# Weight tiles that hold 512 rows of two blocks, and a matmul order that changes block every time

## The chip, the cores and the metric

The kernel runs on one core of a Trainium2 chip. The metric is device time of one execution in microseconds. The engines that matter are TensorE (PE in the profile; its weight loads are listed apart as PEld), VectorE (DVE), ScalarE (ACT), and SyncE (SP), which issues the DMAs.

## The reference, cut to what matters

Two layers of a decoder trunk over 256 positions of width 2048, in float32. What the change touches are the large products of a 256-row activation with a weight matrix:

```
u = rms_norm(x, g_mix);  cq, ckv+rope key, xb, yb, gate_a, gate_r = split(u @ w_in)   # 2048 -> 9280
attn = latent attention(cq, ckv);  rec = gated linear recurrence(xb, yb)
x = x + (sigmoid(gate_a) * attn + sigmoid(gate_r) * rec) @ w_out                     # 2048 -> 2048
x = x + relu(rms_norm(x, g_mlp) @ w_up)^2 @ w_down                                    # 2048 -> 8192 -> 2048
x = x + sigmoid(rms_norm(x, g_ple) @ w_ple_gate) * (p @ w_ple_proj)                   # 2048 -> 2048
```

The result is the final RMSNorm of x after both layers. All weights are used once.

## The kernel before, in words

Activations are stored with features on the 128 partitions and the 256 positions along the free axis, so a product is built from blocks of 128 input rows by 128 output features. An output block is a tile of 128 features x 256 positions in PSUM, summed over 16 blocks of input rows (k = 0 to 15). Float32 accuracy is made of three passes: every weight and every activation is split into a high part, rounded to the matmul's input format, and the low remainder. For each k the helper `mm3` (L219 to L223) issues high weight x high activation (L221), high weight x low activation (L222), low weight x high activation (L223). Each of these is one weight load of 128 x 128 and one matmul with 256 moving columns. The activation buffers bufA and bufB hold, for each k, the high and the low part side by side.

Weights come from HBM as "halves" of 128 x 1024 float32, 512 KB each: one output block by 8 input-row blocks (half s = 0 has k = 0 to 7, half s = 1 has k = 8 to 15). A half goes through four steps. `load` (L102 to L105) issues its DMA on SP into one of six raw buffers, up to eight halves ahead. `split_half` (L116) has ACT copy it to a high tile (L122) and DVE subtract that to get the low tile (L126); there are three buffers of each. `half` (L204) hands the pair to the matmuls and pushes the later halves forward; it also places background jobs of ACT and DVE by an estimate of engine times (E, `work`). `mm_half` (L226) then issues its 24 matmuls, calling `need` for each k, so that the activation block is there.

`mm_pair` (L255) makes two output blocks, t = 0 and t = 1, in the two 256-column parts of one PSUM bank. Its four halves run in the order (t, s) = (0,0) (0,1) (1,0) (1,1). At the first pair of a product, `crossed` swaps the middle two, so that both blocks do k = 0 to 7 before either needs k = 8. Between halves stand hooks, which issue small matmuls of the norms: `root` (L502, tiles `ms`, eight or fewer matmuls of one column) and `spread` (L551, tiles `rb`, a broadcast of the norm factors). The pairs that are not made this way are the last of each product, made by `mm_apart`, the rope key (`mm_tile`), and the small per-head products (tiles k, v, q, qr, lru, pp).

The order of every engine is written out by the program as it runs on the host; there is no scheduler behind it. Stages in a layer: c (compressed q and kv), kr, eight groups of xb, yb, gr, ga and attention, out, then four times up and down, then pg (the last gate).

The lines around the change:

```
        nc.sync.dma_start(out=t, in_=wu[h])                                        # L104
            mm3(o, hi[:, c], lo[:, c], act[0][:, k, 0, :], act[0][:, k, 1, :], first and k == 0, k == 15, shared)  # L234
            t, s = (i % 2, i // 2) if crossed else (i // 2, i % 2)                 # L260
```

## Time and profile before

| | |
|---|---|
| median of 3 runs | 2925.97 us (2925.73 to 2928.0) |
| the profiled execution | 2925.61 us, its span 2923.8 us |
| TensorE busy | 2898.5 us, 99% of the span, 24800 matmuls |
| VectorE, ScalarE busy | 1860.8 us (64%), 1536.2 us (53%) |
| DMA | 535.23 MB, mean 183 GB/s |

The profiled execution spends 1.8 us outside the span that the profile shows. In the profile, matmuls overlap: one lasts about 0.28 us from its start to its end, and the next starts some 0.11 us after it. What a matmul costs is therefore read from the distance of two starts, or from a count over a stretch, not from its length. The busy share of PE says only that a matmul is nearly always in the pipe.

### The profile page before, as it was taken

The page shows a single profiled execution, that of the slowest core. Times are in us where ns is not written, and L with a number is a line of the kernel's source. Part 1 is how long each engine was busy: PE and PEld are TensorE (multiplying, and loading weights), DVE is VectorE, ACT ScalarE, POOL GpSimd, SP SyncE. Part 2 cuts the span into 40 slices and gives each one's busy share as a digit, 9 for nine tenths or more (in the row PEclk, how much of TensorE's full clock was granted, in tenths as well). Part 3 has the DMA queues.
Part 4 walks back from the last instruction along what each step waited for, and adds up shares of the span by engine and source line. Part 5 has one row for each costly group of instructions (what it writes and reads, how often), then busy time and mean ns, then how long its engine had stood idle before and what let it go on. Part 6 is the DMA issues. An engine that isn't in the chain of part 4 may idle for free. (4 is left out here: it accounts for less than half of the span.)

```text
span 2923.8 us, 58376 instructions
## 1 busy us (share of the span) xinstructions
PE 2898.5 (99%) x24800; PEld 2893.3 (99%) x24800; DVE 1860.8 (64%) x2420; ACT 1536.2 (53%) x2050; POOL 8.9 (0%) x17
## 2 busy tenths in 40 slices
PE   8999999999999999999999999999999999999998
PEld 8999999999999999999999999999999999999998
DVE  7877777765455554556758777777654555555565
ACT  5666666644344443444546666665443444434445
POOL 0000000000000000000000000000000000000000
PEclk9999999999999999999999999999999999999999
DMA  6555555555555555555555555555555555555553
GB/s 236 172 179 175 170 177 177 177 195 185 185 187 187 188 187 187 189 186 186 194 182 172 173 174 175 179 180 176 193 187 185 186 187 187 188 188 190 186 183 130
DMA packets 146998, 535.23 MB, mean 183 GB/s; under 512 B 16560, under 2 KB 16816, under 8 KB 146736
## 3 DMA queue, kind: packets, MB, share of 16 engines
q1 hardware_dynamic: 146736, 531.50, 55.2%
q8 instruction: 194, 3.18, 0.4%
q14 instruction: 68, 0.56, 0.0%
HBM read 529.33 MB, written 2.10 MB: 182 GB/s over the span
## 5 line engine op out<-in xcount | busy, mean ns | idle before, releaser
L122 ACT ACTIVATE hi<-raw 128x1024 fp32r<-128x1024 f32 x1004 | 1065.3, 1061 | 1358.5 <-PE down L222 412.0
L126 DVE TENSOR_TENSOR lo<-raw,hi 128x1024 fp32r<-128x1024 f32 x1004 | 1229.2, 1224 | 863.7 <-ACT hi L122 862.2
L221 PE MATMUL down<-bufB,hi 128*128 128x256 f32 x1024 | 287.7, 281 | 0.0
L222 PE MATMUL down<-bufB,hi 128*128 128x256 f32 x1024 | 287.7, 281 | 0.0
L223 PE MATMUL down<-bufB,lo 128*128 128x256 f32 x1024 | 287.7, 281 | 0.0
L221 PE MATMUL down<-bufA,hi 128*128 128x256 f32 x1024 | 287.7, 281 | 0.0
L222 PE MATMUL down<-bufA,hi 128*128 128x256 f32 x1024 | 287.7, 281 | 0.0
L223 PE MATMUL down<-bufA,lo 128*128 128x256 f32 x1024 | 287.7, 281 | 0.0
L221 PE MATMUL up<-bufA,hi 128*128 128x256 f32 x1024 | 287.7, 281 | 0.0
L221 PE MATMUL up<-bufB,hi 128*128 128x256 f32 x1024 | 287.7, 281 | 0.0
L223 PE MATMUL up<-bufA,lo 128*128 128x256 f32 x1024 | 287.5, 281 | 0.0
L223 PE MATMUL up<-bufB,lo 128*128 128x256 f32 x1024 | 287.5, 281 | 0.0
L222 PE MATMUL up<-bufA,hi 128*128 128x256 f32 x1024 | 287.5, 281 | 0.0
L222 PE MATMUL up<-bufB,hi 128*128 128x256 f32 x1024 | 287.5, 281 | 0.0
L222 PEld LDWEIGHTS down<-bufB,hi 128*128 128x128 f32 x1024 | 196.6, 192 | 0.0
L222 PEld LDWEIGHTS down<-bufA,hi 128*128 128x128 f32 x1024 | 196.6, 192 | 0.0
L222 PEld LDWEIGHTS up<-bufB,hi 128*128 128x128 f32 x1024 | 196.4, 192 | 0.0
L222 PEld LDWEIGHTS up<-bufA,hi 128*128 128x128 f32 x1024 | 196.4, 192 | 0.0
L221 PEld LDWEIGHTS up<-bufA,hi 128*128 128x128 f32 x1024 | 192.2, 188 | 0.0
L221 PEld LDWEIGHTS up<-bufB,hi 128*128 128x128 f32 x1024 | 192.2, 188 | 0.0
L223 PEld LDWEIGHTS up<-bufA,lo 128*128 128x128 f32 x1024 | 192.2, 188 | 0.0
L221 PEld LDWEIGHTS down<-bufB,hi 128*128 128x128 f32 x1024 | 192.2, 188 | 0.0
(551 smaller groups left out, 7839.1 us busy)
## 6 DMA issues: line engine op xcount, KB each, us to landing
raw<-wu SPq DMA_DIRECT2D x1004, 512.0 KB, 3.4
y<-rows SPq DMA_DIRECT2D x4, 512.0 KB, 4.0
x<-xT SPq DMA_DIRECT2D x3, 512.0 KB, 8.3
x<-xT SPq DMA_DIRECT2D x2, 256.0 KB, 4.9
praw<-pT SPq DMA_DIRECT2D x2, 256.0 KB, 4.7
parT<-par SPq DMA_DIRECT2D x1, 184.0 KB, 2.4
rope_w<-pos SPq DMA_DIRECT2D x1, 128.0 KB, 3.6
gf<-gfin SPq DMA_DIRECT2D x1, 8.0 KB, 8.3
```

Source lines behind the costliest of these rows:

```text
L122: A.activation(hi, src, AF.Copy)
L126: V.tensor_tensor(out=lo, in0=src, in1=f(hi), op=ALU.subtract)
L221: T.matmul(o, lhsT=wh, rhs=ah, start=start, stop=False, skip_group_check=shared)
L222: T.matmul(o, lhsT=wh, rhs=al, start=False, stop=False, skip_group_check=shared)
L223: T.matmul(o, lhsT=wl, rhs=ah, start=False, stop=stop, skip_group_check=shared)
```

## The change

A raw tile of a pair no longer holds one block by 8 k. It holds both blocks by 4 k: columns 0 to 511 are k = 4i to 4i+3 of block t = 0 and columns 512 to 1023 the same k of block t = 1, for i = 0 to 3. The weights lie in HBM as before; a table, `plan`, says from which two halves each tile is taken, so a tile of a pair is fetched by two DMAs of 128 x 512 (256 KB, rows of 2 KB) in place of one of 128 x 1024 (512 KB, rows of 4 KB). Tiles that are not of a pair are loaded as before. `mm_both` takes the place of `mm_half` in `mm_pair`: for each k it issues six matmuls, high x high, high x low, low x high, each first for t = 0 and then for t = 1, so that the sum written and the weights loaded change at every matmul, and two matmuls after each other read the same activation. `crossed` is gone from the matmul side.

```diff
     def load(h):
         t = wraw.tile([P, 1024], F32, tag="raw", name=f"raw{h}")
-        nc.sync.dma_start(out=t, in_=wu[h])
+        for src, c, n, at in plan[h]:
+            nc.sync.dma_start(out=t[:, at:at + n], in_=wu[src, :, c:c + n])
         raws[h] = t
...
+    def pairs(n, crossed=False):
+
+        for _ in range(n):
+            b = len(plan)
+            for i in range(4):
+                plan.append(tuple(
+                    (b + (2 * (i // 2) + t if crossed else 2 * t + i // 2), 512 * (i % 2), 512, 512 * t) for t in range(2)
+                ))
+            crossed = False
...
+    def mm_both(ps, act, i):
+
+        hi, lo = half()
+        for kk in range(4):
+            k = 4 * i + kk
+            need((act[1], k))
+            ah, al = (act[0][:, k, w, :] for w in range(2))
+
+            for n, (w, a) in enumerate(((hi, ah), (hi, al), (lo, ah))):
+                for t in range(2):
+                    T.matmul(
+                        ps[:, t * S:(t + 1) * S], lhsT=w[:, (4 * t + kk) * P:(4 * t + kk + 1) * P], rhs=a,
+                        start=k == n == t == 0, stop=k == 15 and n == 2, skip_group_check=True,
+                    )
+            E["P"] += 0.656
...
-    def mm_pair(name, key, act, hooks=(), crossed=False):
+    def mm_pair(name, key, act, hooks=()):
 
 
         ps = mm_bank(name, key)
         for i in range(4):
-            t, s = (i % 2, i // 2) if crossed else (i // 2, i % 2)
-            mm_half(ps[:, t * S:(t + 1) * S], act, s, t == 0, True)
+            mm_both(ps, act, i)
             if i < len(hooks) and hooks[i] is not None:
                 hooks[i]()
```

On PE, at the first pair of the product out in layer 0, the last matmuls that wait for the newest activations (k = 14 and 15 of bufB). Before, they stand in the third of the pair's four weight tiles, hi_7052:

```order
L221 MATMUL out_0_7051<-bufB,hi_7052 128x256 [waits Activation_49]
L222 MATMUL out_0_7051<-bufB,hi_7052 128x256 [waits DVE_49]
L223 MATMUL out_0_7051<-bufB,lo_7053 128x256
L221 MATMUL out_0_7051<-bufB,hi_7052 128x256 [waits Activation_49]
L222 MATMUL out_0_7051<-bufB,hi_7052 128x256 [waits DVE_49]
L223 MATMUL out_0_7051<-bufB,lo_7053 128x256
L221 MATMUL out_0_7051<-bufB,hi_7088 128x256
```

In the changed program they stand in the fourth, hi_7237 (equal neighbours are one row with a count; names do not tell the block):

```order
L284 MATMUL out_0_7199<-bufB,hi_7237 128x256 [waits Activation_49]
L284 MATMUL out_0_7199<-bufB,hi_7237 128x256
L284 MATMUL out_0_7199<-bufB,hi_7237 128x256 [waits DVE_49]
L284 MATMUL out_0_7199<-bufB,hi_7237 128x256
L284 MATMUL out_0_7199<-bufB,lo_7238 128x256 x2
L284 MATMUL out_0_7199<-bufB,hi_7237 128x256 [waits Activation_49]
L284 MATMUL out_0_7199<-bufB,hi_7237 128x256
L284 MATMUL out_0_7199<-bufB,hi_7237 128x256 [waits DVE_49]
L284 MATMUL out_0_7199<-bufB,hi_7237 128x256
L284 MATMUL out_0_7199<-bufB,lo_7238 128x256 x2
```

Counted from 0 within the pair's 96 matmuls, the last one that waits (for the low part of k = 15) was number 70 and is now number 92.

On SP, the start of the program. Before, x (the input) and the first weight halves raw_95 and raw_99 are issued so; a wait for a DMAHW semaphore is one for an earlier DMA:

```order
L298 DMA x<-xT 128x512
L104 DMA raw_95<-wu 128x1024
L301 DMA x<-xT 128x512
L301 DMA x<-xT 128x1024
L104 DMA raw_99<-wu 128x1024
L301 DMA x<-xT 128x1024 x2
L304 DMA gf<-gfin 128x16 [waits DMAHW0_49]
L104 DMA raw_140<-wu 128x1024 [waits DMAHW1_49]
```

In the changed program each weight tile takes two issues:

```order
L351 DMA x<-xT 128x512
L142 DMA raw_95<-wu 128x512 x2
L354 DMA x<-xT 128x512
L354 DMA x<-xT 128x1024
L142 DMA raw_100<-wu 128x512 x2
L354 DMA x<-xT 128x1024 [waits DMAHW0_49]
L354 DMA x<-xT 128x1024 [waits DMAHW1_49]
L357 DMA gf<-gfin 128x16 [waits DMAHW2_49]
L142 DMA raw_142<-wu 128x512 [waits DMAHW3_49]
L142 DMA raw_142<-wu 128x512 [waits DMAHW4_49]
```

The first weight tile is complete one issue later, and everything behind it on SP moves back by one issue, behind the second tile by two.

## Rows read from the trace of the kernel before

**Rows 1.** The page's line of busy time by engine (us, share of the span, instructions), and the whole list of PE's waits: who waited for whom, us in total, times, longest.

```profile
PE 2898.5 (99%) x24800; PEld 2893.3 (99%) x24800; DVE 1860.8 (64%) x2420; ACT 1536.2 (53%) x2050; POOL 8.9 (0%) x17
...
PE c L221 <- ACT hi L122: 8.5, 1, 8.5
PE pt L964 <- DVE p L956: 2.6, 2, 1.3
PE ms_fin L502 <- ACT sq_fin L481: 1.6, 1, 1.6
PE s L931 <- DVE qs L852: 1.2, 2, 0.6
PE xt L1216 <- ACT rows L1232: 0.7, 1, 0.7
PE out L222 <- DVE bufA L1024: 0.5, 1, 0.5
PE c L223 <- DVE lo L126: 0.5, 1, 0.5
PE out L222 <- DVE bufB L1024: 0.4, 1, 0.4
```

**Rows 2.** The span cut into stages: start and c; the rest of c and the groups of layer 0; out and the first up pair; up and down; pg; then the same for layer 1 (c and groups together); the last row is the last pg with the end. Columns: stretch, its length, busy us and instructions of PE, PEld, DVE, ACT, POOL, granted clock, DMA share, GB/s.

```profile
0.00:50.00 50.00, 41.07 (x331) 40.73 (x332) 37.32 (x77) 32.36 (x50) 1.80 (x9) 1.00 0.75 266
50.00:545.00 495.00, 493.09 (x4241) 491.29 (x4240) 387.26 (x640) 325.98 (x506) 1.09 (x1) 1.00 0.53 174
545.00:645.00 100.00, 99.56 (x875) 99.36 (x874) 65.60 (x80) 50.59 (x66) 0.00 (x0) 1.00 0.58 190
645.00:1360.00 715.00, 715.00 (x6075) 714.95 (x6074) 384.11 (x377) 311.13 (x341) 0.70 (x1) 1.00 0.58 187
1360.00:1470.00 110.00, 110.00 (x967) 109.95 (x966) 78.13 (x99) 58.64 (x78) 0.70 (x1) 1.00 0.59 192
1470.00:2002.00 532.00, 530.08 (x4554) 528.22 (x4554) 400.47 (x626) 340.83 (x524) 2.56 (x2) 1.00 0.53 175
2002.00:2094.00 92.00, 91.47 (x807) 91.27 (x807) 58.89 (x69) 46.36 (x60) 0.00 (x0) 1.00 0.58 194
2094.00:2808.00 714.00, 714.00 (x6066) 713.95 (x6065) 383.16 (x376) 311.49 (x340) 0.70 (x1) 1.00 0.57 187
2808.00:2924.00 116.00, 104.21 (x904) 103.60 (x902) 65.91 (x79) 58.84 (x92) 1.39 (x2) 0.97 0.44 150
```

**Rows 3.** PE's instructions in order of time (start us, length us, line, operation, out<-in): two from the stage out, 84 matmuls apart, and two from the stage up, also 84 apart.

```profile
569.89 0.28 PE L221 MATMUL out<-bufB,hi 128*128 128x256 f32 x1
...
579.41 0.28 PE L221 MATMUL out<-bufB,hi 128*128 128x256 f32 x1
...
699.95 0.28 PE L221 MATMUL up<-bufA,hi 128*128 128x256 f32 x1
...
709.85 0.28 PE L221 MATMUL up<-bufA,hi 128*128 128x256 f32 x1
```

**Rows 4.** The same view around the two hooks at the first two up pairs of layer 0: the hook's own matmuls, and one close behind each; between the hooks four matmuls that follow each other.

```profile
646.73 0.50 PE L502 MATMUL ms_mlp<-ones,nacc_mlp 128*128 128x1 f32 x4
647.10 0.37 PE L221 MATMUL up<-bufA,hi 128*128 128x256 f32 x1
...
654.67 0.28 PE L221 MATMUL up<-bufA,hi 128*128 128x256 f32 x1
654.79 0.28 PE L222 MATMUL up<-bufA,hi 128*128 128x256 f32 x1
654.90 0.28 PE L223 MATMUL up<-bufA,lo 128*128 128x256 f32 x1
655.01 0.28 PE L221 MATMUL up<-bufA,hi 128*128 128x256 f32 x1
...
655.36 0.59 PE L551 MATMUL rb_mlp<-dg_mlp,ones 128*128 128x256 f32 x2
...
655.90 0.28 PE L222 MATMUL up<-bufA,hi 128*128 128x256 f32 x1
```

**Rows 5.** The same view in the first out pair, where PE waits; in brackets the idle time and what ended it. The first four are of layer 0, the others of layer 1. From the first row of each four to the second there are 72 matmuls in layer 0 and 66 in layer 1.

```profile
547.07 0.28 PE L221 MATMUL ga<-bufA,hi 128*128 128x256 f32 x1
...
555.55 0.28 PE L221 MATMUL out<-bufB,hi 128*128 128x256 f32 x1
556.27 0.39 PE L222 MATMUL out<-bufB,hi 128*128 128x256 f32 x1 [0.44 <-DVE bufB L1024]
556.49 0.28 PE L223 MATMUL out<-bufB,lo 128*128 128x256 f32 x1
...
1995.47 0.28 PE L221 MATMUL out<-bufA,hi 128*128 128x256 f32 x1
...
2002.95 0.28 PE L221 MATMUL out<-bufA,hi 128*128 128x256 f32 x1
2003.76 0.39 PE L222 MATMUL out<-bufA,hi 128*128 128x256 f32 x1 [0.53 <-DVE bufA L1024]
2003.98 0.28 PE L223 MATMUL out<-bufA,lo 128*128 128x256 f32 x1
```

**Rows 6.** The same view at three small products of layer 0: the first matmul of qr (12 matmuls into one sum), of lru (12 matmuls, four sums of three each; the activation of the last matmul of one sum is the first one's of the next, twice) and of ga.

```profile
106.52 0.28 PE L221 MATMUL qr<-c0hi,hi 128*128 128x256 f32 x1
...
107.92 0.28 PE L221 MATMUL lru<-xc_0h,hi 128*128 128x256 f32 x1
...
109.32 0.28 PE L221 MATMUL ga<-bufA,hi 128*128 128x256 f32 x1
```

**Rows 7.** DMA: the main queue (packets, MB, share of 16 engines); from the issues, the weights' DMA (count, size, median us to landing); from the waits, ACT's for weights that had not landed, and SP's for a free raw buffer (us in total, times, longest).

```profile
q1 hardware_dynamic: 146736, 531.50, 55.2%
...
raw<-wu SPq DMA_DIRECT2D x1004, 512.0 KB, 3.4
...
ACT hi L122 <- DMA raw<-wu: 2.0, 3, 1.2
...
SPq L104 <- DVE lo L126: 2295.8, 928, 4.9
```

**Rows 8.** SP's issues and ACT's first work in order of time (start us, length us, line, operation).

```profile
1.66 0.42 SPq L104 DMA_DIRECT2D raw<-wu  x1
2.13 0.91 SPq L301 DMA_DIRECT2D x<-xT  x2
...
7.35 1.06 ACT L122 ACTIVATE hi<-raw 128x1024 fp32r<-128x1024 f32 x1 [1.22 <-DMA raw<-wu]
```

More of the change, by code (lines that the diff above doesn't have):

```diff
@@ L100, in trunk_kernel, with alone @@
     LA, PD = 2, 8
+    plan = []
+    def alone(n):
+        for _ in range(n):
+            plan.append(((len(plan), 0, 1024, 0),))
+    def pairs(n, crossed=False):
+        for _ in range(n):
+            b = len(plan)
[4 more added lines that the diff above has]
+            crossed = False
+    for _ in range(DEPTH):
+        pairs(4, True)
+        alone(2)
+        for g in range(GROUPS):
+            pairs(3 if g == 0 else 2)
+            alone(4)
+            pairs(1 if g in (0, GROUPS - 1) else 2)
+            if g == GROUPS - 1:
+                alone(4)
+        pairs(7, True)
+        alone(4)
+        for _ in range(CHUNKS):
+            pairs(8, True)
+            pairs(7, True)
+            alone(4)
+        for i in range(4):
+            alone(1)
+            pairs(2 if i < 3 else 1, i == 0)
+        alone(4)
     def load(h):
         t = wraw.tile([P, 1024], F32, tag="raw", name=f"raw{h}")
-        nc.sync.dma_start(out=t, in_=wu[h])
+        for src, c, n, at in plan[h]:
+            nc.sync.dma_start(out=t[:, at:at + n], in_=wu[src, :, c:c + n])
         raws[h] = t
@@ L224, in mm3, with mm_half @@
         E["P"] += 0.328
-    def mm_half(o, act, s, first=True, shared=False):
+    def mm_half(o, act, s):
         hi, lo = half()
@@ L233, in mm_half @@
             c = slice(kk * P, (kk + 1) * P)
-            mm3(o, hi[:, c], lo[:, c], act[0][:, k, 0, :], act[0][:, k, 1, :], first and k == 0, k == 15, shared)
+            mm3(o, hi[:, c], lo[:, c], act[0][:, k, 0, :], act[0][:, k, 1, :], k == 0, k == 15)
+    def mm_both(ps, act, i):
[11 more added lines that the diff above has]
+            E["P"] += 0.656
     readers = {}
@@ L644, in mixer @@
             key = ("c", i, pr, l)
-            ps = mm_pair(f"c{i}{pr}_{l}", key, u, hooks.get(n, ()), n == 0)
+            ps = mm_pair(f"c{i}{pr}_{l}", key, u, hooks.get(n, ()))
             later(key, ("A", 0.6, lambda i=i, pr=pr, ps=ps: A.activation(dest(i, pr), ps, AF.Copy)), rank=-1)
@@ L1049, in residual @@
                 keys = (f"{name}_{pr}",)
-                ps = mm_pair(f"{name}_{pr}", keys[0], act, (), pr == 0)
+                ps = mm_pair(f"{name}_{pr}", keys[0], act)
                 later(keys[0], ("V", 0.65, lambda ps=ps, pr=pr: add(ps, pair_of(x, pr))), rank=-1)
@@ L1065, in mlp @@
                     (ple_fetch, ple_rows)[pr // 5](l)
-                ps_u = mm_pair(f"up{nm}", ("up", nm), a, BOUNDARY.get(8 * c + pr, lambda n: ())(norm), pr == 0)
+                ps_u = mm_pair(f"up{nm}", ("up", nm), a, BOUNDARY.get(8 * c + pr, lambda n: ())(norm))
                 def steps(ps, pr, nm):
@@ L1148, in ple @@
                 hook = BOUNDARY[pr](norm) if pr < 2 else hooks(pr)
-                ps = mm_pair(f"pg{nm}", ("pg1", nm), a, hook, pr == 0)
+                ps = mm_pair(f"pg{nm}", ("pg1", nm), a, hook)
                 scale, tanh, mul, add = steps(ps, pps[pr % 2], pair_of(x, pr), lambda nm=nm: t512(f"pgt{nm}"))
```

## The prediction

> **What bounds the kernel now.** I read the line of busy times first, then PE's waits, then the stages, and last PE's instructions one by one. The busy line shows PE at work for 2898.5 of 2923.8 us with 24800 matmuls, while DVE and ACT are at 64% and 53%. The list of waits is complete: PE waits 16.0 us in all, 8.5 of them for the first weights [rows 1]. So the time is the number of matmuls times their distance, plus some 25 us, and only the distance is left to look at.
>
> That distance has two values, though the granted clock is 1.00 in every stage but the last, which ends at 0.97 [rows 2]. In the stage out, 84 matmuls take 9.52 us, 113.3 ns each. In up, 84 matmuls of the same shape take 9.90 us, 117.9 ns each [rows 3]. The stages say the same: 6075 matmuls in 715.00 us and 6066 in 714.00 us are 117.7 ns throughout up and down [rows 2]. I call them the fast pace and the slow pace; they differ by about 4.5 ns, 4%.
>
> What chooses the pace is the question on which this change hangs. Three rows speak to it. Ahead of the norm's one-column matmuls and behind them PE runs fast; behind the two broadcast matmuls `rb` at 655.36 it runs slow [rows 4], and stays slow for the 704 us until pg. Weights, activations and order are alike on both sides. In layer 0 PE enters out at the slow pace, 72 matmuls in 8.48 us (117.8 ns). It waits once for the last activation, and runs fast from there [rows 5, 3]. In layer 1 it came in fast (66 matmuls in 7.48 us, 113.3 ns) and left fast. So the pace is a state in which PE stays until something breaks the stream, and the same instructions run in either.
>
> The third row bears on the new order itself. In qr twelve matmuls add into one sum; in lru the sum changes every third matmul, and twice two neighbours read the same activation. Both take 1.40 us [rows 6]. A change of sum or a repeated activation costs and gains nothing there, within the 0.01 us of a row. What the row doesn't have is such a change at every matmul.
>
> **The change part by part.** The number of matmuls stays, and so does the number of weight loads: every matmul had its own before, also where L222 repeats L221's weights. What changes at each matmul is which of two sums is written, that weights never repeat, and that activations repeat in twos. Bounds: at the fast end all 24800 at 113.3 ns are 2810 us, with 25.3 us of idle time and 1.8 us outside the span 2837, which is 88 below the profiled 2925.6. At the slow end no row is slower than the slow pace for long; if every fast stretch went slow, the 875 + 967 + 807 matmuls of rows 2 outside up, down and groups, the 904 of the last stage and the first 331 would lose 4.5 ns each, 17 us, and the groups, whose 8795 matmuls are at 116.3 ns on the mean, at most 13 more. I take zero, the value of the row nearest to the new order (qr against lru).
>
> The hook `rb` stands where it stood, behind the third weight tile of the second pair, with PE fast before it. So I let up and down start slow again, in both layers: 0.
>
> The waits in out move. `crossed` had k = 15 needed at matmul 70 of the first pair; now it is number 92. PE lost there, against its pace, 0.72 + 0.22 - 0.24 = 0.70 us in layer 0 and 0.81 + 0.22 - 0.23 = 0.80 us in layer 1 [rows 5]. Twenty-two matmuls later is 2.6 us later, so both waits go: -1.5 us. But in layer 0 that wait was also what broke the slow pace. Without it the slow pace lasts until the one-column matmuls at 646.73 [rows 4]: from 556.49 that is 90.1 us, 795 matmuls, 4.5 ns each: +3.6 us. In layer 1 PE was fast already and stays so: 0. What is late next is nothing: k = 14 is needed one group of six earlier and was ready.
>
> The loads. Each of 872 pair tiles takes two issues in place of one. On SP an issue takes 0.47 us with its spacing (1.66 to 2.13) [rows 8]; 410 us more over the span lie inside the 2295.8 us that SP waits for raw buffers [rows 7]. At the start nothing covers it: the first weights are complete one issue later, ACT's first high copy waited for them, and PE for that [rows 8, 1]: +0.5 us. The second tile and the x chunks behind it come up to 0.9 us later, but are needed 24 or more matmuls later; I take 0, at most 1.
>
> The packets halve from 4 KB to 2 KB. One takes 0.552 x 16 x 2923.8 us / 146736 = 176 ns of a DMA engine now [rows 7]. If a 2 KB packet takes half, the share stays 0.58 in up and down; if it took the whole 176 ns, the share would be 1.16 and DMA would be the bound there. The nearest rows say that landing has room: 3.4 us from issue to landing, up to eight tiles ahead, and ACT waited for weights only 2.0 us in the whole run [rows 7]. I take half, so 0. [...]
>
> ACT and DVE wait for two DMA semaphores where one was, at the first reader of each tile. In up and down they idle half of the time [rows 2]; in the groups ACT is busy 326 of 495 us and PE's waits there are 4 us in all [rows 1]. Zero, at most 2 us.
>
> Sum on the profiled execution: 2925.6 + 3.6 - 1.5 + 0.5 = 2928.2, say 2928. The profiled execution lies 0.4 us under the median of the runs, which changes nothing.
>
> **The rivals.** First, the order or the entry gives the fast pace where it was slow. Up and down are 12141 matmuls; at 4.5 ns, 55 us, so 2873, and 2900 if only one layer turns; with the slow parts of the groups too, down to the 2837 above. For it: the fast pace exists, for the same shapes, without any idle time to fill, and the pace after `rb` has no reason that I can read from the rows, so a different neighbour might turn it. Against it: `rb` led to the slow pace in each stage whose rows I read, and the sum's change did nothing in lru.
>
> Second, on the other side, the new order can't hold the fast pace: two matmuls in a row stream the same activation block while a new weight block is loaded each time, and fast stretches all had a repeated weight block at every third matmul. Price: the 17 us above to 30, thus 2943 to 2956. It decides as soon as stretches like out and pg show 117.8. Against it: at the fast pace the matmul that repeats weights and those that don't come at the same distance, 0.11 to 0.12 us each [rows 4], so the repetition isn't what it lives on.
>
> Third, the DMA becomes the bound in up and down: with 2 KB packets above 176 / 1.16 = 152 ns the share reaches 1. At 176 ns, 0.16 of 1429 us and of some 400 us in out and pg: 295 us, thus about 3220. For it: nothing but that the price of a 2 KB packet is not in the trace. Against it: the room at landing.
>
> That the change doesn't do what it says is excluded by the order: the sums do alternate, and the second waiting place is where I put it. Whether it matters to PE is what the first two rivals ask.
>
> **How the numbers follow.** The forecast, paces as before, has 0.68: 2921 to 2937, since in 14 groups and in pg the pace after a short wait falls either way (208 matmuls at 4.5 ns are 0.9 us each time). The first rival has 0.19, two thirds of it under 2890; the second 0.09; the third 0.02; other mixtures 0.02. A measurement of this kernel can tell about 0.2%, 5.9 us, from no change: 2920.1 and 2931.8. Faster: 0.19 and 0.02 of the forecast's own, 0.21. Slower: 0.12 of rivals and mixtures, and a quarter of the forecast's share, together 0.29. The same: 0.50. The range leaves out 0.08 below, where everything turns fast, and 0.08 above: 2868 to 2944.
>
> **What would show it.** Right: 84 matmuls in 9.90 us in up and down, no wait of PE at out, and in layer 0 about 9.9 us for 84 matmuls in out; the first high copy of ACT at about 7.8; ACT's waits for weights still under some 5 us. Wrong: a distance of 113 ns in up (first rival), 118 in pg and both outs (second), or any distance that the trace before doesn't have; DMA shares near 1 and long waits of ACT for `raw` (third). A distance between 109 and 113 ns would show that the alternation acts on PE in a way that no row of before could tell.

## The result, and the profile after

The changed kernel takes 2883.3 us (median of 4 runs, 2881.9 to 2884.1) against 2925.9 us (4 runs) for the kernel before: ratio 0.985, 95% interval 0.984 to 0.987. It is 42.5 us faster, 1.5%, where the prediction had 2928 us and no change. The profiled execution has a span of 2880.1 us and took 2881.9 us.

The page's line of busy time and the whole list of PE's waits in the changed kernel (us in total, times, longest):

```profile
PE 2853.1 (99%) x24800; PEld 2846.8 (99%) x24800; DVE 1861.3 (65%) x2420; ACT 1538.4 (53%) x2050; POOL 10.1 (0%) x17
...
PE c L284 <- ACT hi L160: 8.6, 1, 8.6
PE pt L1017 <- DVE p L1009: 2.6, 2, 1.3
PE ms_fin L555 <- ACT sq_fin L534: 1.6, 1, 1.6
PE c L284 <- DVE bufA L637: 1.5, 2, 0.8
PE c L284 <- ACT bufA L633: 1.3, 1, 1.3
PE xt L1269 <- ACT rows L1285: 0.7, 1, 0.7
PE s L984 <- DVE qs L905: 0.6, 2, 0.3
PE c L284 <- DVE lo L164: 0.3, 1, 0.3
```

PE has as many matmuls as before and is again 99% busy. Its waits are 17.2 us, 1.2 more than in [rows 1]: the two waits at out are gone, and three short ones in the first c pair have come. So the gain isn't in the waits. It is in the distance of the matmuls. The same two stretches as in [rows 2], up and down of either layer, with the same columns:

```profile
645.00:1360.00 715.00, 715.00 (x6301) 714.95 (x6300) 398.63 (x395) 323.17 (x353) 1.39 (x2) 1.00 0.59 194
2094.00:2808.00 714.00, 713.25 (x6288) 712.96 (x6287) 399.82 (x396) 325.78 (x361) 0.70 (x1) 1.00 0.59 194
```

6301 and 6288 matmuls stand where 6075 and 6066 stood, at the same granted clock of 1.00. That is 448 matmuls more in the same time, some 51 us at the fast pace. By the spans the gain is 43.7 us, so some 7 us have been lost elsewhere.

PE's instructions in order of time, as in [rows 3]: two rows of out and two of up, 84 matmuls apart (a row x4 holds the two high products of both sums, the row x2 between them the low ones, so from one row x4 to the next there are six matmuls):

```profile
569.66 0.63 PE L284 MATMUL out<-bufB,hi 128*128 128x256 f32 x4
...
579.56 0.64 PE L284 MATMUL out<-bufB,hi 128*128 128x256 f32 x4
...
699.84 0.62 PE L284 MATMUL up<-bufA,hi 128*128 128x256 f32 x4
...
709.36 0.62 PE L284 MATMUL up<-bufA,hi 128*128 128x256 f32 x4
```

No new distance has come: 9.52 us (113.3 ns a matmul) and 9.90 us (117.9 ns) are the two values of [rows 3], but they have changed places. Up is fast now, and out is slow. The page shows it without counting as well: its groups by shape give 276 ns as the mean length of an up or down matmul, and 281 ns of one in out; before, up and down had 281.

The hooks at the first two up pairs, as in [rows 4]:

```profile
653.05 0.50 PE L555 MATMUL ms_mlp<-ones,nacc_mlp 128*128 128x1 f32 x4
...
654.21 0.64 PE L284 MATMUL up<-bufA,hi 128*128 128x256 f32 x4
...
661.27 0.63 PE L284 MATMUL up<-bufA,hi 128*128 128x256 f32 x4
...
661.98 0.59 PE L604 MATMUL rb_mlp<-dg_mlp,ones 128*128 128x256 f32 x2
...
663.80 0.62 PE L284 MATMUL up<-bufA,hi 128*128 128x256 f32 x4
...
670.60 0.62 PE L284 MATMUL up<-bufA,hi 128*128 128x256 f32 x4
```

Between the hooks 60 matmuls take 7.06 us (117.7 ns), behind rb 60 take 6.80 us (113.3 ns). In [rows 4] it is the other way round: fast behind ms, slow behind rb. At all eight ms and all eight rb of the two layers the starts of the matmuls say the same, in the kernel before and in the changed one. So the question for the runs is what turned the hooks over.

### The profile page after: what moved, and what is told of

It reads as the page before. It is cut to its first block, busy times and chain, and to the rows that moved or that the text cites. A ratio compares the mean times of both kernels' runs of the same rounds, so it can differ in the third digit from the quotient of the medians.

```text
span 2880.1 us, 60564 instructions
## 1 busy us (share of the span) xinstructions
PE 2853.1 (99%) x24800; PEld 2846.8 (99%) x24800; DVE 1861.3 (65%) x2420; ACT 1538.4 (53%) x2050; POOL 10.1 (0%) x17
## 2 busy tenths in 40 slices
DMA packets 272583, 535.43 MB, mean 186 GB/s; under 512 B 30512, under 2 KB 30768, under 8 KB 272304
## 3 DMA queue, kind: packets, MB, share of 16 engines
q1 hardware_dynamic: 272304, 531.55, 55.6%
## 4 chain that ended last, share of the span: by engine, by line
PE 98%; ACT 1%; DVE 0%; DMA 0%; issue 0%; SPq 0%; ACTq 0%; POOLq 0%
PE up L284 24%; PE down L284 21%; PE yb L284 6%; PE gr L284 6%; PE xb L284 6%; PE out L284 5%; PE pg L284 5%; PE ga L284 5%; PE c L284 3%; PE down L259 1%; PE down L260 1%; PE down L261 1%; PE o L1040 1%; PE s L984 1%; PE v L872 1%; PE v L873 1%
## 5 line engine op out<-in xcount | busy, mean ns | idle before, releaser
L160 ACT ACTIVATE hi<-raw 128x1024 fp32r<-128x1024 f32 x1004 | 1065.7, 1061 | 1311.6 <-DMA raw<-wu 467.4
L284 PE MATMUL up<-bufA,hi 128*128 128x256 f32 x2048 | 316.2, 276 | 0.0
L284 PE MATMUL up<-bufB,hi 128*128 128x256 f32 x2048 | 316.2, 276 | 0.0
L284 PE MATMUL down<-bufB,hi 128*128 128x256 f32 x1792 | 276.0, 276 | 0.0
L284 PE MATMUL down<-bufA,hi 128*128 128x256 f32 x1792 | 276.0, 276 | 0.0
L284 PEld LDWEIGHTS up<-bufA,hi 128*128 128x128 f32 x2048 | 270.6, 188 | 0.1
L284 PEld LDWEIGHTS up<-bufB,hi 128*128 128x128 f32 x2048 | 270.6, 188 | 0.1
L284 PEld LDWEIGHTS down<-bufB,hi 128*128 128x128 f32 x1792 | 236.4, 188 | 0.0
L284 PEld LDWEIGHTS up<-bufB,lo 128*128 128x128 f32 x1024 | 154.3, 188 | 0.0
L284 PEld LDWEIGHTS down<-bufA,lo 128*128 128x128 f32 x896 | 134.9, 188 | 0.0
L284 PEld LDWEIGHTS down<-bufB,lo 128*128 128x128 f32 x896 | 134.8, 188 | 0.0
```

The source lines that it names most:

```text
L160: A.activation(hi, src, AF.Copy)
L284: T.matmul(ps[:, t * S:(t + 1) * S], lhsT=w[:, (4 * t + kk) * P:(4 * t + kk + 1) * P], rhs=a, start=k == n == t == 0, stop=k == 15 and n = ...
```

## The experiments

Each kernel was timed against the kernel before on the same chip. In this table stands, beside time and ratio, the number of matmuls that the view by stretches counts in out (560 to 640 us) and in up and down (700 to 1300 us): 708 and 5297 are the fast pace, 682 and 5097 the slow one. The last column is explained further down.

| kernel | us | ratio to before (95%) | out | up, down | nacc |
|---|---|---|---|---|---|
| before | 2925.9 | | 708 | 5096 | 32 |
| changed | 2883.3 | 0.985 (0.984 to 0.987) | 682 | 5297 | 0 |
| e1_blockwise | 2879.1 | 0.984 (0.981 to 0.987) | 708 | 5296 | 0 |
| e2_no_repeat | 2925.5 | 1.000 (0.999 to 1.002) | 708 | 5097 | 32 |
| e3_lo_before_al | 2881.2 | 0.985 (0.982 to 0.988) | 682 | 5296 | 0 |
| e4_two_k | 2928.7 | 1.001 (1.000 to 1.003) | 709 | 5097 | 32 |
| e5_packed | 2878.5 | 0.984 (0.982 to 0.985) | 682 | 5297 | 0 |
| e6_two_loads | 2925.7 | 1.000 (0.999 to 1.001) | 708 | 5097 | 32 |
| e7_first_load | 2924.6 | 1.000 (0.999 to 1.001) | 708 | 5097 | 32 |
| e8_by_twelve | 2883.3 | 0.984 (0.980 to 0.988) | 682 | 5297 | 0 |
| e9_columns | 2928.6 | 1.001 (1.000 to 1.002) | 708 | 5097 | 32 |
| e10_crossed | 2924.7 | 1.000 (0.999 to 1.001) | 708 | 5097 | 32 |
| e11_nacc_at_0 | 2870.9 | 0.982 (0.980 to 0.983) | 708 | 5297 | 0 |
| e12_nacc_at_32 | 2936.8 | 1.004 (1.003 to 1.006) | 681 | 5097 | 32 |
| e13_before_aligned | 2868.9 | 0.981 (0.980 to 0.983) | 708 | 5297 | 0 |
| e14_after_aligned | 2874.6 | 0.983 (0.981 to 0.984) | 708 | 5296 | 0 |
| e15_dg_at_32 | 2935.7 | 1.004 (1.002 to 1.005) | 675 | 5097 | 32 |
| e16_both_moved | 2880.6 | 0.985 (0.983 to 0.987) | 701 | 5296 | 0 |
| e17_column_at_32 | 2869.3 | 0.980 (0.979 to 0.982) | 708 | 5296 | 0 |
| e18_column_at_0 | 2871.9 | 0.981 (0.980 to 0.983) | 708 | 5297 | 0 |

**The order of the matmuls (e1 to e4, e8).** The change's headline is that the two sums take turns. The first runs took it apart.

e1_blockwise, the changed kernel with its two inner loops exchanged:

```diff
-            for n, (w, a) in enumerate(((hi, ah), (hi, al), (lo, ah))):
-                for t in range(2):
+            for t in range(2):
+                for n, (w, a) in enumerate(((hi, ah), (hi, al), (lo, ah))):
```

> The changed kernel's loads and tiles, but for each k the three matmuls of block 0 and then the three of block 1, so that weights repeat again (high, high, low) and the sum changes only every third matmul. If the order of the matmuls chose the pace (theories 'repeat' and 'sums'), up and down are back at 117.8 ns per matmul behind the broadcast matmuls, and the time is 2925 to 2935 us. If the loads or what they do to ACT and DVE chose it (theory 'loads'), up and down stay at 113.3 ns and the time stays at 2882 to 2886 us.

e2_no_repeat, the kernel before with its three products in another order:

```diff
-            mm3(o, hi[:, c], lo[:, c], act[0][:, k, 0, :], act[0][:, k, 1, :], first and k == 0, k == 15, shared)
+            ah, al = (act[0][:, k, w, :] for w in range(2))
+            for n, (w, a) in enumerate(((hi, ah), (lo, ah), (hi, al))):
+                T.matmul(o, lhsT=w[:, c], rhs=a, start=first and k == n == 0, stop=k == 15 and n == 2, skip_group_check=shared)
```

> The kernel before, with its loads and one sum per half, and the order high x high, low x high, high x low for each k: no weight block is loaded twice in a row, two neighbours read the same activation, and the sum does not change. Theory 'repeat' (the pace is chosen by whether a weight block repeats): up and down at 113.3 ns, 2868 to 2885 us. Theory 'sums' (it is chosen by the sum's change at each matmul): 117.8 ns as before, 2922 to 2932 us. Theory 'loads': as before too, 2922 to 2932 us.

e3_lo_before_al, the same in the changed kernel:

```diff
-            for n, (w, a) in enumerate(((hi, ah), (hi, al), (lo, ah))):
+            for n, (w, a) in enumerate(((hi, ah), (lo, ah), (hi, al))):
```

> The changed kernel with the second and third pass swapped: for each k high x high of both blocks, low x high of both, high x low of both. Sums change at each matmul and no weight block repeats, as in the changed kernel; four neighbours read the same activation. Theories 'repeat', 'sums' and 'loads' all say 113.3 ns in up and down and 2880 to 2888 us. If the pace behind a hook is so sensitive that any other order turns it, up and down may be at 117.8 ns, some 2930 to 2940 us.

e4_two_k, the kernel before with two row blocks interleaved, so that neighbours never share a weight block, within one sum:

```diff
-        for kk in range(8):
+        for kk in range(0, 8, 2):
...
+            for n, (w, part) in enumerate(((hi, 0), (hi, 1), (lo, 0))):
+                for j in range(2):
```

> The kernel before, with its loads and one sum per half, and two k taken together: high x high of both, high x low of both, low x high of both. No weight block repeats, no activation repeats, and the sum does not change. Theory 'repeat': up and down at 113.3 ns, 2868 to 2885 us. Theories 'sums' and 'loads': 117.8 ns, 2922 to 2932 us. Were it the repeated activation that matters, this one is slow and the one with high, low, high is fast.

e8_by_twelve, the changed kernel with twelve matmuls of one block, then twelve of the other in each tile:

```diff
-        for kk in range(4):
-            k = 4 * i + kk
+        for t in range(2):
+            for kk in range(4):
+                k = 4 * i + kk
```

> The changed kernel with its loads and tiles, but within a tile first the twelve matmuls of the first block, then the twelve of the second: the sum changes twice a tile, not at every matmul. If the fine alternation of the two halves of the PSUM bank (every matmul or every third) sets which pace follows a hook (theory 'alternation'), the paces fall back to those of the kernel before: some 2925 to 2932 us, fast behind ms, slow behind rb. If it is enough that both halves of the bank are advanced within a tile (theory 'tiles'), the paces are the changed kernel's: 2879 to 2885 us.

Every order made out of the changed kernel has fast up and down, every order made out of the kernel before has slow ones. Neither the turns nor the repeated weight block sets the pace.

**The loads (e5 to e7).** e5_packed lays the pair tiles out on the host as the changed kernel wants them:

```diff
-        for src, c, n, at in plan[h]:
-            nc.sync.dma_start(out=t[:, at:at + n], in_=wu[src, :, c:c + n])
+        nc.sync.dma_start(out=t, in_=wu[h])
```

> The changed kernel's matmuls in their order, with its tiles (two blocks of features by four row blocks), but packed so on the host: each tile comes in one 512 KB DMA. If what stands in the tiles or the order of the matmuls turns the paces over (theory 'tiles'), the time is that of the changed kernel, about 2883 us, slow behind ms and fast behind rb. If the second DMA of each pair tile does it (theory 'two DMAs'), or the second DMA of the first tile alone does it (theory 'first load': it comes ahead of PE's first matmul and moves the number of the counter that PE raises from 108 to 109), the paces are those of the kernel before: about 2926 to 2931 us, fast behind ms, slow behind rb.

e6_two_loads splits the loads of the kernel before, e7_first_load only the very first (in e6, n is 512 for each tile of a pair):

```diff
-        nc.sync.dma_start(out=t, in_=wu[h])
+        n = 512 if h == 0 else 1024
+        for c in range(0, 1024, n):
+            nc.sync.dma_start(out=t[:, c:c + n], in_=wu[h, :, c:c + n])
```

> The kernel before, its tiles and matmuls untouched, but each tile of a pair comes in two DMAs of 128x512. Theory 'two DMAs': the paces turn over, slow behind ms, fast behind rb, some 2880 to 2885 us. Theory 'first load' says the same. Theory 'tiles': as before, 2926 us.

> The kernel before with one edit: the very first weight tile comes in two DMAs of 128x512; the other 1003 in one. Theory 'two DMAs': as before, 2926 us, fast behind ms, slow behind rb. Theory 'first load': the paces turn over for the whole run, some 2880 to 2885 us, with PE's counter at 109 in the rows. Theory 'tiles': as before, 2926 us.

The loads don't set it either. What the changed kernel shows of them, from the page and from ACT's waits:

```profile
q1 hardware_dynamic: 272304, 531.55, 55.6%
...
raw<-wu SPq DMA_DIRECT2D x1744, 256.0 KB, 3.0
...
ACT hi L160 <- DMA raw<-wu: 467.4, 284, 2.2
```

Nearly twice the packets of [rows 7] take the same share of the DMA engines, 55.6% against 55.2%. ACT's 467.4 us are no cost. In e6, the kernel before with two loads a tile, ACT waits 418.2 us for weights where it had waited 2.0, and yet all its waits together are 1375.1 us in both: the same idle time is put down to another releaser. PE's own waits for weights are the two at the start of c in the list above, 8.6 and 0.3 us.

**The place of the hooks (e9, e10).** e9_columns puts two one-column matmuls behind rb, since ms, which is made of such, was followed by the fast pace before:

```diff
+            if self.parts == 1:
+                for j in range(2):
+                    T.matmul(rb[:, w + j:w + j + 1], lhsT=self.dg[:, j * P:(j + 1) * P], rhs=ones[:, 0:1], start=True, stop=True)
```

> The kernel before, with two one-column matmuls, like those of ms, behind the two broadcast matmuls rb of each norm but the small one; what they write is never read. Every ms of the kernel before is followed by the fast pace. If the pace is set by the last short matmuls ahead of the stream and stays (theory 'restart'), up and down turn fast: 12000 matmuls less 4.5 ns, 54 us, some 2873 us. If something else around rb decides, such as the state of ACT and DVE there, nothing changes but half a microsecond at each: 2926 to 2930 us.

e10_crossed takes every pair crossed, with the weights laid out on the host to suit, so that rb stands between other tiles:

```diff
-            t, s = (i % 2, i // 2) if crossed else (i // 2, i % 2)
+            t, s = i % 2, i // 2
```

> The kernel before with its loads, but each pair, not only a stage's first, takes its tiles crossed: rows 0 to 7 of both blocks, then rows 8 to 15 of both. So both halves of the bank are advanced by turns of 24 matmuls, and the hook rb, behind the third tile, now stands between other tiles. Theory 'alternation' and theory 'tiles' (four rows of both in one tile): as before, some 2925 us. If it is the tile at which the hook rb stands, or the bank that is left half done there (theory 'place'), the paces may turn over: some 2873 to 2885 us.

Both stay as the kernel before. After ten runs all that the diff says had been excluded, and yet four kernels ran like the changed one and six like the one before. The last three matmuls ahead of ms and the first three behind it are the same instructions in e1 and before, with the same waits. What they don't share is an address. The layout that the builds give, in bytes within a partition:

```
                                   invf     nacc, two tiles
before, e2, e4, e6, e7, e9, e10    108704   104608, 106656   (32 past a multiple of 64)
changed, e1, e3, e5, e8            104608   104640, 106688   (multiples of 64)
```

nacc is the tile of squares that ms reads as its weights. invf is a tile of 4 bytes a partition; in the second line nacc lies 32 bytes behind it. In both lines the tiles lie in the order in which the program first makes them. nacc is made by the first square that the planner emits, invf by rope_tables, behind the first c pair. In the kernel before the planner had emitted a square by then; in the changed one it had not. So invf comes first, and nacc lies 32 bytes further on. (invf has moved as well, but PE doesn't read it: DVE does, for the rope tables.)

**The place of nacc alone (e11, e12).** e11_nacc_at_0 makes invf early in the kernel before; no instruction changes:

```diff
     hbx = const.tile([P, DEPTH, 16], F32, name="hbx")
+    fr = const.tile([P, 1], F32, name="invf")
...
     def rope_tables():
-        fr = const.tile([P, 1], F32, name="invf")
```

> The kernel before, with no instruction changed: only the 4-byte tile invf is laid out first, so that the nacc tiles, which ms reads as weights, move by 32 bytes, from 104608 and 106656 (32 past a multiple of 64) to 104640 and 106688 (multiples of 64), as in the changed kernel. Theory 'place': ms is followed by the slow pace, rb turns that into the fast one, up and down are fast: 2879 to 2886 us. Theory 'order' (something in the changed order that the runs so far did not separate): as before, 2925 us.

e12_nacc_at_32 puts it back in the changed kernel, where invf goes into spare bytes of the tile power:

```diff
-    power = const.tile([P, 4], F32, name="power")
+    small = const.tile([P, 8], F32, name="power")
+    power = small[:, 0:4]
...
-        fr = const.tile([P, 1], F32, name="invf")
+        fr = small[:, 4:5]
...
+                    const.tile([P, 1], F32, tag="pad", name=f"pad_{self.name}")
```

> The changed kernel with its order and loads, only invf lies in spare bytes of another tile, so that nacc is at 104608 and 106656 as in the kernel before; all other tiles that PE reads stay where they are. Theory 'place': fast behind ms, slow behind rb, up and down slow: 2925 to 2933 us (out may be slow in both layers, 3.6 us). Theory 'order': as the changed kernel, 2883 us.

The hooks in e11, the kernel before with nacc moved:

```profile
645.97 0.50 PE L502 MATMUL ms_mlp<-ones,nacc_mlp 128*128 128x1 f32 x4
...
647.12 0.28 PE L221 MATMUL up<-bufA,hi 128*128 128x256 f32 x1
...
654.19 0.28 PE L221 MATMUL up<-bufA,hi 128*128 128x256 f32 x1
...
654.89 0.60 PE L551 MATMUL rb_mlp<-dg_mlp,ones 128*128 128x256 f32 x2
...
656.36 0.28 PE L221 MATMUL up<-bufA,hi 128*128 128x256 f32 x1
...
663.84 0.28 PE L221 MATMUL up<-bufA,hi 128*128 128x256 f32 x1
```

And in e12, the changed kernel with nacc put back:

```profile
653.69 0.50 PE L556 MATMUL ms_mlp<-ones,nacc_mlp 128*128 128x1 f32 x4
...
654.84 0.62 PE L284 MATMUL up<-bufA,hi 128*128 128x256 f32 x4
...
661.63 0.62 PE L284 MATMUL up<-bufA,hi 128*128 128x256 f32 x4
...
662.32 0.59 PE L605 MATMUL rb_mlp<-dg_mlp,ones 128*128 128x256 f32 x2
...
664.16 0.63 PE L284 MATMUL up<-bufA,hi 128*128 128x256 f32 x4
...
671.23 0.63 PE L284 MATMUL up<-bufA,hi 128*128 128x256 f32 x4
```

In e11, 60 matmuls behind ms take 7.07 us (117.8 ns) and 66 behind rb 7.48 us (113.3 ns), as in the changed kernel. In e12, 60 take 6.79 us behind ms (113.2 ns) and 7.07 us behind rb (117.8 ns), as in the kernel before. Thirty-two bytes decide it, in both directions, and they are worth 54 us in e11 and 53 us between e12 and the changed kernel. e9 doesn't speak against it: the columns behind its rb read dg, which lies at multiples of 64, and the slow pace follows; but it would have followed without them too.

The two also give what the change itself does, with nacc at the same place: e12 against before is 1.004 (1.003 to 1.006), 12 us slower; the changed kernel is 12 us slower than e11, measured in different sets of runs. That is also why both times miss the ranges that I had set, e11 by 8 us below and e12 by 4 us above: I had left most of this cost out.

**The rest of the slow pace (e13, e14).** The small products of the groups read tiles at 32 past a multiple of 64 too. Both kernels get a larger xbuf, which moves these to multiples of 64; e13_before_aligned has e11's edit as well:

```diff
-    xbuf = att.tile([P, 2, 260], F32, name="xbuf")
+    room = att.tile([P, 2, 264], F32, name="xbuf")
+    xbuf = room[:, :, 0:260]
```

> e11, and the tile xbuf is 32 bytes larger, so that the tiles behind it, which the small products k, q, qr, v, lru and pp read, move from 32 past a multiple of 64 to multiples of 64; no instruction changes. If operands at 32 past a multiple of 64 are what makes PE slow (theory 'place', for the groups too): the small products run at 113.3 ns in place of 116.7, the groups and out stay fast, and only the 66 matmuls behind each ms are slow: 24800 at 113.3 ns and some 30 us, 2838 to 2855 us. If the place of nacc is an accident of its own and the groups have another reason: 2875 to 2886 us.

> The changed kernel with the larger xbuf of e13. Theory 'place', for the groups too: 2838 to 2855 us, some 30 to 45 us less than the changed kernel. Else 2875 to 2886 us. Against e13 it gives what the change itself costs or gains once the places are alike: nothing over 0.2% if the order has no effect.

e13 is 2 us below e11, with overlapping intervals, and e14 9 us below the changed kernel, with intervals that just touch. The large gain in the groups that I expected isn't there: they still change between both paces. Yet some of the small products did turn as expected. In every kernel up to e12, q, qr and lru take 116.7 ns a matmul, 1.40 us for twelve as in [rows 6]; in e13 and e14 they take 113.3, 1.36 us for twelve. In e13, the first matmuls of qr and of lru, 12 apart:

```profile
104.45 0.28 PE L221 MATMUL qr<-c0hi,hi 128*128 128x256 f32 x1
...
105.81 0.28 PE L221 MATMUL lru<-xc_0h,hi 128*128 128x256 f32 x1
```

But k stands at 117.8 ns, and the matmuls of gr behind lru, fast in 13 of e11's 14 groups that have them there, are slow in all 14. So what was gained in the one place was lost in the other. Where e14 is faster than the changed kernel, part of it is out, which it enters fast: 708 matmuls in 80 us for 682. Against e13, in the same set of runs, e14 is 5.6 us slower: with these places the change itself costs 0.2%.

**What rb does, and the rule of ms elsewhere (e15 to e18).** In all kernels rb is followed by the pace opposite to the one ahead of it. e15_dg_at_32 and e16_both_moved (with e11's edit) move dg, the operand of rb, to 32 past a multiple of 64:

```diff
+    tmp.tile([P, 1], F32, tag="pad", bufs=1, name="pad_t")
+    att.tile([P, 1], F32, tag="pad", name="pad_a")
```

> The kernel before with two unused 32-byte tiles, so that dg, the moving operand of rb, and the other temporaries move from multiples of 64 to 32 past one, while the small products' operands stay at 32 past one and nacc stays at 32 past one. Theory 'flip' (rb turns over whatever pace enters it): as before, fast behind ms, slow behind rb, about 2925 us. Theory 'own place' (the pace behind a hook comes from the place of that hook's own operand, 32 for fast, 0 for slow): fast behind ms and behind rb, about 2866 to 2872 us.

> e15 with nacc at multiples of 64, as in e11. Theory 'flip': as e11, slow behind ms, fast behind rb, about 2871 us. Theory 'own place': slow behind ms, fast behind rb, the same 2871 us; only a slow pace behind rb, some 2925 to 2931 us, would speak against both, and for a rule in which the two places act together.

With dg at either place, slow follows fast and fast follows slow (up and down have 5097 matmuls in 600 us in e15, 5296 in e16): rb turns the pace over. Both are about 10 us slower than with dg at its old place. By the traces 9 of them lie in the groups of the two layers (9.6 us from kr to out in e15 against before, 8.8 in e16 against e11). There q, qr and lru take 120.0 ns a matmul in place of 116.7. In e15:

```profile
106.09 0.28 PE L221 MATMUL qr<-c0hi,hi 128*128 128x256 f32 x1
...
107.53 0.28 PE L221 MATMUL lru<-xc_0h,hi 128*128 128x256 f32 x1
```

Their operands have moved along by 64 bytes, xc from 180448 to 180512 and c from 198880 to 198944, and lie at 32 past a multiple of 64 as before. So for these products the remainder by 64 can't be all that counts.

e17_column_at_32 and e18_column_at_0 put one one-column matmul ahead of each group's first xb matmul, in e11. By the rule taken from ms a single column, too, would set the pace by the place of its weights: fast with mask, at 32 past a multiple of 64, and slow with ident, at a multiple of 64.

```diff
+        if name.startswith("xb"):
+            T.matmul(ps[:, 0:1], lhsT=mask[:, 0:P], rhs=ones[:, 0:1], start=True, stop=True)
```

In e18 the weights are those of ident in place of mask.

> e11, with one one-column matmul ahead of each group's first xb matmul (16 in all); its weights are read from mask, which lies at 101024, 32 past a multiple of 64, and the next matmul overwrites what it writes. [...] If the place matters in ms alone, or something else that moved with nacc: 3 to 4 us more than e11, about 2874 us.

> e17, but the weights of the one-column matmuls are read from ident, which lies at 99968, a multiple of 64. By the rule: slow from there to k in all 16 groups, also where e11 came in fast; e11 and 16 x 0.23 us, 2874 to 2877 us. If the break in the stream is what matters and not the place: as e17.

In e17, at group 2 of layer 0, where PE comes in slow:

```profile
186.79 0.28 PE L221 MATMUL ga<-bufA,hi 128*128 128x256 f32 x1
...
187.50 0.28 PE L221 MATMUL ga<-bufA,hi 128*128 128x256 f32 x1
...
187.85 0.28 PE L260 MATMUL xb<-ones,mask 128*128 128x1 f32 x2
...
188.31 0.28 PE L223 MATMUL xb<-bufA,lo 128*128 128x256 f32 x1
...
188.99 0.28 PE L223 MATMUL xb<-bufA,lo 128*128 128x256 f32 x1
```

In e18, at the same place, and at group 4, where PE comes in fast and the column stands at 307.21:

```profile
186.27 0.28 PE L223 MATMUL ga<-bufA,lo 128*128 128x256 f32 x1
...
186.98 0.28 PE L223 MATMUL ga<-bufA,lo 128*128 128x256 f32 x1
...
187.10 0.28 PE L260 MATMUL xb<-ones,ident 128*128 128x1 f32 x2
...
187.91 0.28 PE L223 MATMUL xb<-bufA,lo 128*128 128x256 f32 x1
...
188.93 0.28 PE L223 MATMUL xb<-bufA,lo 128*128 128x256 f32 x1
...
305.50 0.28 PE L221 MATMUL ga<-bufA,hi 128*128 128x256 f32 x1
...
306.86 0.28 PE L221 MATMUL ga<-bufA,hi 128*128 128x256 f32 x1
...
307.66 0.28 PE L223 MATMUL xb<-bufA,lo 128*128 128x256 f32 x1
...
308.72 0.28 PE L223 MATMUL xb<-bufA,lo 128*128 128x256 f32 x1
```

In e17 six matmuls ahead of the column take 0.71 us (118 ns), six behind it 0.68 (113 ns). So it is at 14 of the 16 groups, 13 of which come in slow and one fast; the two others (group 1 of each layer) are followed by the slow pace; there the column doesn't follow a stream but stands behind short products. In e18 the column turns the pace over: at group 2, slow in (six in 0.71 us), nine take 1.02 us behind it (113.3 ns); at group 4, fast in (twelve in 1.36 us), nine take 1.06 us (117.8 ns). Ten turn from slow to fast, four from fast to slow, and behind the same two the pace is slow. So what a column reads as its weights matters outside the norm too, most likely by its place (mask and ident also differ in what they hold: zeros there, and a unit matrix). But my rule for multiples of 64, "slow", was wrong for a single column.

Nor does that rule hold for ms without exception. nacc lies at multiples of 64 in e17 and e18 too; yet three of their sixteen ms (the first ms_mix in e17, both ms_c in e18) are entered at the slow pace and left at the fast one. The first ms_c of e18:

```profile
63.63 0.28 PE L221 MATMUL xb<-bufA,hi 128*128 128x256 f32 x1
...
65.04 0.28 PE L221 MATMUL xb<-bufA,hi 128*128 128x256 f32 x1
...
65.40 0.95 PE L504 MATMUL ms_c<-ones,nacc_c 128*128 128x1 f32 x8
...
66.64 0.28 PE L221 MATMUL xb<-bufA,hi 128*128 128x256 f32 x1
...
69.36 0.28 PE L221 MATMUL xb<-bufA,hi 128*128 128x256 f32 x1
```

Twelve matmuls ahead of it take 1.41 us (117.5 ns), 24 behind it 2.72 us (113.3 ns). The rb behind each of these three is then entered fast and left slow. So rb goes by the pace that enters it, whatever the place of nacc.

The time disappoints. By the rule I had priced e17 at some 9 us below e11: in 14 groups 195 matmuls at 4.5 ns, 0.87 us, less 0.23 us for the column. The 0.23, which stands in the price of e18 too, is half of the 0.45 us that ms adds in the kernel before (646.62 to 647.30 us from the last matmul ahead of ms to the second behind it, less two steps of the fast pace). e17 is 1.6 us below e11 and e18 1.0 above, in other sets of runs and with overlapping intervals. In e17 what xb and yb gain is partly given back: the matmuls from lru into gr, fast in these groups of e11, are slow, and the columns themselves cost some 0.22 us each. In its profiled execution, which took 5 us more than the other three, out of layer 1 is slow as well (90.95 us to the first up matmul, against 88.05 in e11). Of all kernels run, e13, e17, e11 and e18 are the fastest, and their intervals don't part them; the simplest is e11, the kernel before with one tile made earlier. It is faster than the kernel before and than the changed one.

## Why the prediction was wrong

**What bounds the kernel: right.** The time is 24800 matmuls times their distance; in the large products the distance has two values, which came out as 113.3 and 117.8 ns again in every kernel; and the pace is a state that lasts until something breaks the stream. But "two values" left out a third: the 1.40 us for twelve matmuls in [rows 6] are 116.7 ns, neither of the two.

**The step that failed** is this: "The hook `rb` stands where it stood, behind the third weight tile of the second pair, with PE fast before it. So I let up and down start slow again, in both layers: 0." PE was not fast before it. The pace behind ms had turned, because nacc lay 32 bytes further on, and rb turned it over once more. The term was 448 matmuls' time, some 51 us, with the sign of a gain. I read the pace behind a hook as belonging to the hook. Rows 4 allowed two readings, "rb makes it slow" and "rb turns it over", and I weighed only the first. The layout of tiles I didn't compare at all: neither the diff nor the order of instructions shows an address.

**The first rival** had nearly the right time (2873 us; the range down to 2868 holds the result only because it took most of this rival in) and the wrong mechanism for the most part: "the order or the entry gives the fast pace". Its doubt was right, that the pace behind rb "has no reason that I can read from the rows". The order had no part in it (e1 to e4, e8); the entry into rb had.

**out: half right.** Both waits went, as predicted. In layer 0 the slow pace then lasted to ms, as predicted: 682 matmuls in 80 us against 708. (The stretch that I took as 90.1 us is 646.73 - 556.49 = 90.24; the term stays 3.6.) For layer 1 I wrote "PE was fast already and stays so: 0"; it came in slow this time, since the groups ahead of it fell otherwise, and stayed slow. In both layers that is some 2.5 us each, by the time from the first out to the first up matmul (90.5 us against 88.1 and 87.9).

**The start: mis-sized.** I gave 0.5 us, and up to 1 for the later tiles. In the kernel before ms_mix starts at 39.52 us, in e12 at 43.93: 4.4 us. The list of waits above has three new ones, all for bufA, 2.8 us together. It is not the second load that I priced; ACT's first copy starts at 7.51 us for 7.35, where I had 7.8. e5, with one load a tile, has the same waits for bufA (1.5 and 1.3 us) and ms_mix at 42.80, against 42.73 in the changed kernel; e6, with two loads a tile, has it at 38.63. In the seven kernels with the new tiles ms_mix starts between 42.73 and 46.80 us, in the thirteen with the old ones between 38.47 and 40.44. So it comes with the new order of the rows, k by k for both blocks. By what way it makes the high and low copies late wasn't tried.

**DMA: right.** That a packet of half the size takes half the time was my estimate, and no row of the kernel before showed it. The 272304 packets of the changed kernel take 94 ns of an engine each on the mean, where I had worked out 176 before: the share of the engines, times the span, is 1601 us for 1614. ACT's waits for weights were to stay under some 5 us; the view has 467.4, but at no cost, as said above. Here 256 KB a DMA in place of 512 cost nothing that shows: e6, with two loads a tile and nothing else changed, has a ratio of 1.000 (0.999 to 1.001).

**The second rival, lost pace in the new order, fell.** Both outs came out slow, which was one of its signs; but with the sums taking turns at each matmul, up and down hold 113.3 ns over 600 us (5297 matmuls).

Put together, with nacc in its old place the change costs 12 us (e12), where I had 2.6: the start was 3.9 us short and out of layer 1 some 3.4. That makes 9.9 us. The two profiled executions lie 10.2 us apart; why the medians lie 2 us further apart no trace shows.

## What to carry to other kernels

Where matmuls stand shoulder to shoulder, compare their start-to-start distance by stage in both traces before believing any story about order or loads; a few per cent (here 113.3 or 117.8 ns a matmul) can hang on a state into which a single odd matmul puts the engine, as in e17 and e18. A change that makes tiles in another order can move addresses, as it moved nacc by 32 bytes here: print the layout of both builds, and undo the shift alone, before giving the gain to the edit. Here 32 bytes gave 54 us, and the edit itself cost 12, or 6 with e13's places.

## What the runs showed of the hardware

- A stream of matmuls of 128x256 f32 has two lasting paces at a granted clock of 1.00, 113.3 and 117.8 ns from start to start. It held one of them for 600 us, with no wait between (5096 matmuls in the kernel before, 5297 in the changed one). In the short products q, qr and lru, whose operands move with xbuf, the distance was 113.3 (e13, e14), 116.7 or 120.0 ns (e15, e16), by the place of those operands.
- The one-column matmuls of ms (two or four, each of which stands as two in the trace: rows x4 and x8) change the pace by where their weights lie. With nacc at 32 past a multiple of 64 the fast pace followed at all 72 places ahead of the end (nine kernels, eight places each), whichever pace came in. With nacc at a multiple of 64 the slow one followed at 85 of 88 (eleven kernels): at all 72 entered fast, and at 13 of 16 entered slow. A single one sets fast at 32 (e17), and at a multiple of 64 it turns the pace over (e18), each at 14 of 16 groups. rb turns it over (117.7 to 113.3 ns in the changed kernel, 113.2 to 117.8 in e12), with dg at either place. Why, no view shows, nor what parts the three from the thirteen.
- nacc was tried at two places alone, 32 bytes apart; with the one or the other the matmuls behind ms differ by 4% (113.2 ns in e12, 117.7 in the changed kernel). That 64 is the divisor that counts is not shown.
- A short wait is no sure way to the fast pace. Behind the longest wait in out (0.2 to 0.5 us) it followed at 23 of 26 places in the thirteen kernels that have this wait, the slow pace at three (one each in e4, e15 and e17).
- Open: what sets the pace with which gr goes on behind lru, and so why the operands of the small products, moved to multiples of 64 in e13, changed the time of the groups so little in sum.
